# Output stage of a hybrid decoder layer: row tiles in another order of products and transposes

## Chip, core and metric

The kernel runs on one core of a Trainium2 chip. The metric is the device time of one execution in microseconds (us); the median of the runs shown is compared. Five engines work side by side, each through its own list of instructions in order: PE (TensorE, matrix products and transposes), DVE (VectorE), ACT (ScalarE), POOL (GpSimd) and SP (SyncE, which here only issues DMA transfers). An instruction that waits for a semaphore holds up everything behind it on its engine.

## The reference, cut to what matters

One layer on 1024 tokens (and 16 meta tokens) of width 1024. Two head groups, a gated delta rule (GDN) and a forgetting attention (FOX), give 512 columns each; their outputs are concatenated and go through one output projection, a residual add, an RMSNorm and a SwiGLU FFN.

```python
h = h + jnp.concatenate([o_gdn, o_fox], axis=-1) @ w_out[l]        # the output stage
h = h + swiglu(rmsnorm(h, ffn_norm_w[l]), w_gate[l], w_up[l], w_down[l])
h = rmsnorm(h, final_norm_w)
return h[:, N_META:]
```

All is float32. Each product is made of three: an operand is split into a rounded high part and the rest, and hi*hi, hi*lo and lo*hi are summed (`mm3`). `split` makes the two parts, the high one by a cast on ACT, the low one by a subtraction on DVE behind it.

## The kernel before

The stages follow each other: input projection and GDN, attention, output stage, FFN, down projection with the final norm. The change lies in the output stage and in its passage to the FFN (some 620 to 745 us of the profile below).

**The output stage** works on eight row tiles of 128 tokens, in the order `ORDER` = 0, 4, 1, 5, 2, 6, 3, 7; columns go in two halves of 512 (`nb` 0 and 1). The GDN part of half 0 is done in the attention stage for all tiles. For a tile `tt`:

- `prep_load` (L1111) loads the attention output `of` from DRAM on SP (L1113), lets POOL add its two partial halves (L1114), and lets ACT write the reciprocal row sums into the freed half (L1115).
- `prep_pe` (L1119) transposes these on PE (`rbt`, four transposes, L1125), multiplies on DVE (L1126) and splits the result into `ohl` (ACT L160, DVE L161).
- `load_h` (L1131) loads the residual `hst` on SP: for the tiles in `fused` (4, 5, 2, 6, 3, 7) one half from the input x and one from `h_d`, else all from `h_d`.
- `fox_g` (L1142) computes for a fused tile the GDN part of half 1 into the one PSUM bank `mm` (`wx`, 12 products of 128x512).
- `out_fox` (L1152) computes the FOX part, 12 products, for half 0 into `wof`, for half 1 on top of `wx` (or into `wof`). DVE adds the residual (`hst`, L1158). After half 1 comes the norm: a square sum on ACT (L1051), a scale on DVE (L205), a power on POOL (`st_f`, L206), the scaled row on DVE (`xn`, L1053).
- `u_blocks` (L1217) transposes the normed tile on PE (`u2t`, eight transposes, L1224) and splits it, or sums and differences of two tiles, into the FFN's operands `uh`, `ul` (ACT and DVE, two of the six low parts and one difference, `br`, on POOL).

Tiles have two buffers each for `of`, `hst`, `ohl` and `xn2`, so a tile's load waits until the tile two places before is done with the buffer. On PE the order is the order of the code (`tc.manual_schedule`); on the other engines a scheduler places the instructions by the code's order and its own costs. `tc.issue_after(ins)` holds back what stands in its block until `ins` has been placed.

```python
for i, tt in enumerate(ORDER):           # L1385, i = 0 is done before the loop
    if i > 1: fox_g(tt)
    out_fox(tt, 0)
    ... prep_pe(ORDER[i + 1]); load_h(ORDER[i + 1]); prep_load(ORDER[i + 2])
    out_fox(tt, 1)
    if i < NT - 1: u_blocks(ORDER[i - 1])   # at i = 7 it stands ahead of out_fox(tt, 1)
```

**Before the loop** (L1170 to L1187) tiles 0 and 4 are started: `wout_block` (L1062) loads and splits the four weight blocks of the FOX part. The last of them, `wf`, are written by ACT and DVE into memory from which the attention's last outputs `oa` are still being stored to DRAM (`o_d`). `wog` is here the GDN part of half 1 of tile 1, which is not fused; `fox_g` of tile 4 (`wx`) follows it on PE.

**The FFN** takes 11 steps `j`; a step needs seven products `p1`, `p6`, `p2`, `p7`, `p5`, `p4`, `p3` for the gate (g) and the up weights (u), with sums of weight blocks as operands. `w_ops` (L1274) makes the sums (`ws`, `s`) and splits on DVE and ACT, `ffn_bank` the products (`ga`, `ua`, `gb`, `ub`, ...: L1311, 12 each), `ffn_evict` (L1340) takes them out of PSUM (DVE L1355, `gxy`, `uxy`, `gzw`, `uzt`).

## Time and profile before

| | us |
|---|---|
| median of 3 runs | 1351.39 (1350.51 to 1355.45) |
| the profiled execution | 1359.66 |
| its span, first to last instruction | 1358.0 |
| PE busy in the span | 1312.7 (97%) |
| DVE, ACT, POOL busy | 855.4, 558.9, 430.4 |
| mean granted clock of PE | 0.983 of full speed |

The profile is one execution; the rows further down are from it. It gives for each engine when an instruction ran and what ended the idle time ahead of it. PE is busy nearly all the time, so what counts is where PE waits and where its granted clock is not 1.00; work on another engine matters where PE waits for it.

### The profile page before, as it was taken

The numbers are of one execution on the slowest core, as the hardware profiler recorded it, in microseconds if no ns is written. First come the engines' busy times: TensorE is split into PE (matmuls) and PEld (weight loads), VectorE is DVE, ScalarE is ACT, GpSimd is POOL, SyncE is SP. The second block draws the span as 40 slices with busy tenths as digits, with TensorE's granted clock in tenths as the row PEclk, the third lists the DMA queues.
The fourth block names the chain that finished last, engine by engine and source line by source line (L and its number), as shares of the span: only waits on it lengthen the run. The fifth ranks groups of instructions, "written<-read, shape, count | busy, mean of one in ns | idle before, by whom it ended". The sixth has DMA issues, their size and how long they took to land.

```text
span 1358.0 us, 20228 instructions
## 1 busy us (share of the span) xinstructions
PE 1312.7 (97%) x7442; PEld 1144.6 (84%) x7442; DVE 855.4 (63%) x1503; ACT 558.9 (41%) x930; POOL 430.4 (32%) x414
## 2 busy tenths in 40 slices
PE   8999998999999999998988999999999999999997
PEld 7999998989989877886767888888888888888886
DVE  5565677858536577994677566566655565455645
ACT  6453455322223466883444333333323343334332
POOL 2111034211022155661331654334444553010301
PEclk8999999999999998999998999999999999999999
DMA  7121536595579697846443444444455447954523
GB/s 245 57 73 53 145 113 186 164 249 168 157 271 309 172 279 206 208 114 195 146 155 117 146 171 157 160 157 164 155 171 179 165 145 254 404 224 171 199 80 124
DMA packets 192954, 237.93 MB, mean 175 GB/s; under 512 B 18896, under 2 KB 144712, under 8 KB 189144
## 3 DMA queue, kind: packets, MB, share of 16 engines
q1 hardware_dynamic: 192856, 236.65, 54.3%
q8 instruction: 58, 0.95, 0.3%
q14 instruction: 40, 0.33, 0.1%
HBM read 159.00 MB, written 77.60 MB: 174 GB/s over the span
## 4 chain that ended last, share of the span: by engine, by line
PE 80%; DMA 7%; DVE 5%; issue 3%; POOL 2%; ACT 2%; SPq 1%; POOLq 0%; DVEq 0%; ACTq 0%
PE xp L1472 8%; PE yp L1472 7%; PE ud L1311 4%; PE gd L1311 4%; PE gb L1311 4%; PE ub L1311 4%; PE ua L1311 4%; PE ga L1311 4%; PE pj_fk L200 3%; PE pj_fq L200 3%; PE ue L1311 2%; PE ge L1311 2%; PE pt L973 2%; PE fv L200 1%; PE pq L473 1%
## 5 line engine op out<-in xcount | busy, mean ns | idle before, releaser
L161 DVE TENSOR_TENSOR al_p<-ra_p,ah_p 128x2048 fp32r<-128x2048 f32 (+1 forms) x21 | 46.6, 2221 | 93.9 <-ACT ah_p L160 93.9
L926 POOL TENSOR_TENSOR bi<-ccol,cr 128x144 f32<-128x144 f32 (+7 forms) x60 | 69.7, 1166 | 55.1 <-DVE sm L942 36.1
L160 ACT CAST ah_p<-ra_p 128x2048 fp32r<-128x2048 f32 (+1 forms) x21 | 37.1, 1766 | 105.7 <-PE xp L1472 48.5
L1472 PE MATMUL xp<-wh_p,ah_p 128*128 128x512 f32 (+1 forms) x187 | 70.5, 377 | 0.7 <-DVE hs L1499 0.7
L1472 PE MATMUL xp<-wl_p,ah_p 128*128 128x512 f32 (+1 forms) x187 | 70.4, 377 | 0.0
L1472 PE MATMUL xp<-wh_p,al_p 128*128 128x512 f32 (+1 forms) x187 | 70.4, 376 | 0.0
L1360 POOL TENSOR_TENSOR gzw<-gzw,uzt 128x512 f32<-128x512 f32 x11 | 18.5, 1685 | 159.2 <-DVE uzt L1355 147.9
L1311 PE MATMUL gb<-uh_p,w_g_p 128*128 128x512 f32 x176 | 59.0, 397 | 2.9 <-DVE gxy L1355 2.9
L1360 POOL TENSOR_TENSOR gxy<-gxy,uxy 128x512 f32<-128x512 f32 x22 | 36.8, 1672 | 67.6 <-DVE uxy L1355 54.2
L1311 PE MATMUL ub<-uh_p,w_u_p 128*128 128x512 f32 x176 | 57.8, 389 | 0.0
L1311 PE MATMUL gd<-uh_p,w_g_p 128*128 128x512 f32 x176 | 57.7, 389 | 0.0
L1311 PE MATMUL ud<-uh_p,w_u_p 128*128 128x512 f32 x176 | 57.7, 389 | 0.0
L161 DVE TENSOR_TENSOR pl<-pt,ph 128x512 fp32r<-128x512 f32 (+1 forms) x96 | 51.8, 551 | 5.7 <-ACT ph L160 5.1
L161 DVE TENSOR_TENSOR w_u_p<-raw_u,w_u_p 128x512 fp32r<-128x512 f32 x42 | 41.6, 990 | 20.6 <-ACT w_u_p L160 20.5
L947 ACT ACTIVATE pr<-pr,sm 128x144 f32<-128x144 f32 (+3 forms) x64 | 50.5, 789 | 9.8 <-DVE sm L942 8.8
L160 ACT CAST ph<-pt 128x512 fp32r<-128x512 f32 (+1 forms) x96 | 45.2, 472 | 21.3 <-PE pt L973 20.8
L1311 PE MATMUL ga<-uh_p,w_g_p 128*128 128x512 f32 x160 | 52.5, 389 | 0.0
L1311 PE MATMUL ua<-uh_p,w_u_p 128*128 128x512 f32 x160 | 52.5, 389 | 0.0
L1472 PE MATMUL yp<-wh_p,ah_p 128*128 128x512 f32 x132 | 51.3, 389 | 0.0
L1472 PE MATMUL yp<-wl_p,ah_p 128*128 128x512 f32 x132 | 51.3, 389 | 0.0
L1472 PE MATMUL yp<-wh_p,al_p 128*128 128x512 f32 x132 | 51.3, 389 | 0.0
L160 ACT CAST w_u_p<-raw_u 128x512 fp32r<-128x512 f32 x42 | 26.0, 620 | 57.8 <-PE gd L1311 41.5
(629 smaller groups left out, 4350.0 us busy)
## 6 DMA issues: line engine op xcount, KB each, us to landing
ra_p<-ao_p SPq DMA_DIRECT2D x14, 1024.0 KB
raw_g<-in_w_gate_dram SPq DMA_DIRECT2D x22, 512.0 KB
raw_u<-in_w_up_dram SPq DMA_DIRECT2D x22, 512.0 KB
raw_d<-in_w_down_dram SPq DMA_DIRECT2D x22, 512.0 KB
wt_p<-raw_d SPq DMA_DIRECT2D x33, 256.0 KB
rw_p<-wt_p SPq DMA_DIRECT2D x8, 1024.0 KB
kk<-k_d SPq DMA_DIRECT2D x14, 520.0 KB
rw_p<-in_w_down_dram SPq DMA_DIRECT2D x6, 1024.0 KB
```

The lines of the kernel that those rows point to most:

```text
L160: cast = nc.scalar.copy(dst_hi, src)
L161: tail[0] = (cast, nc.vector.tensor_sub(dst_lo, src, dst_hi.bitcast(F32)))
L200: nc.tensor.matmul(dst, a, b, start=first, stop=last)
L473: nc.tensor.matmul(pq[:, 256 * i:256 * i + 256], kq[:, 0, c:c + P], kq[:, :, c:c + P], start=True, stop=True)
L926: nc.gpsimd.tensor_tensor(bi[:, :n], ccol[:, h, j:j + 1].broadcast_to([P, n]), cr[:, :n], op=ALU.subtract)
L947: nc.scalar.activation(pr[:, :n], pr[:, :n], AF.Exp, bias=sm[:, np_ - 1:np_], scale=-1.0, accum_out=rsum[:, h, j:j + 1])
L973: nc.tensor.transpose(pt[:rows_k, P * j:P * j + P], pts[j][0][:, c0:c0 + rows_k], ident)
L1311: nc.tensor.matmul(dst, a[:, c], b[:, k], start=(first and k == 0 and i == 0), stop=(k == 3 and i == 2), skip_group_check=not first)
L1360: last_mul[0] = G.tensor_tensor(gs[d], gs[d], us[d], op=ALU.mult)
L1472: nc.tensor.matmul(dst[:, n_], a[:, f, c], b[:, f, n_], start=(first and i == 0 and n == 0), stop=(i == NF - 1 and n == 2), skip_group_che ...
```

## The change

No product, transpose or transfer is added or removed. The order changes:

- Before the loop the transposes of tile 0 go ahead of `fox_g` of tile 4, those of tile 4 between the two halves of tile 0. The split of the last `wf` blocks is held back behind the split `ohl` of tile 0. The loads of `hst` for tiles 0 and 4 and of the norm's weights `nwb` are held back behind the load of `of` for tile 4.
- In the loop `fox_g(tt)` and, for the tiles from the fourth on, `u_blocks` of the tile before go between the two halves of tile `tt`.
- The first weight sums of the FFN (j = 0) are held back behind the last residual add, those of j = 1 and its first split behind the evictions of `p5` of j = 0.

```diff
     prep_load(ORDER[0])
     with tc.issue_after(last_o[0].ins):
+        prep_load(ORDER[1])
+    with tc.issue_after(ofl[ORDER[1]].ins):
         nc.sync.dma_start(nwb2, ffn_norm_w[0].partition_broadcast(P))
-    prep_load(ORDER[1])
...
-    wfs = [wout_block(4, 0), wout_block(4, 1, lambda i: [pf_tile(2 * i + c, f"wf{c}_{i}") for c in range(2)])]
+    wfs = [wout_block(4, 0)]
     rot[0] = 1
     for _ in wout_gdn(1, 1):
         pass
+    first_o = prep_pe(ORDER[0])
+    with tc.issue_after(first_o[0].ins), tc.issue_after(first_o[1].ins):
+        wfs.append(wout_block(4, 1, lambda i: [pf_tile(2 * i + c, f"wf{c}_{i}") for c in range(2)]))
+    with tc.issue_after(ofl[ORDER[1]].ins):
+        load_h(ORDER[0])
     fox_g(ORDER[1])
-    prep_pe(ORDER[0])
-    load_h(ORDER[0])
     prep_load(ORDER[2])
     out_fox(ORDER[0], 0)
+    prep_pe(ORDER[1])
+    with tc.issue_after(ofl[ORDER[1]].ins):
+        load_h(ORDER[1])
     out_fox(ORDER[0], 1)
-    prep_pe(ORDER[1])
-    load_h(ORDER[1])
     prep_load(ORDER[3])
...
+    def after_p5(j):
+        es = ExitStack()
+        for ins in p5s if j == 1 else ():
+            es.enter_context(tc.issue_after(ins.ins))
+        return es
...
-            V.tensor_tensor(s3, a11, a21, op=ALU.subtract)
-            V.tensor_tensor(a21, a21, a22, op=ALU.add)
-            V.tensor_tensor(s2, a21, a11, op=ALU.subtract)
-            V.tensor_tensor(s4, a12, s2, op=ALU.subtract)
+            with after_p5(j):
+                V.tensor_tensor(s3, a11, a21, op=ALU.subtract)
+                V.tensor_tensor(a21, a21, a22, op=ALU.add)
+                V.tensor_tensor(s2, a21, a11, op=ALU.subtract)
+                V.tensor_tensor(s4, a12, s2, op=ALU.subtract)
...
-                w_split(m, j, p, src)
+                with after_p5(j if p == "p1" else 0):
+                    w_split(m, j, p, src)
...
         for i, tt in enumerate(ORDER):
             if not i:
                 continue
-            if i > 1:
-                fox_g(tt)
             out_fox(tt, 0)
-            if i == NT - 1:
-                u_blocks(ORDER[i - 1])
-            else:
+            if i < NT - 1:
                 prep_pe(ORDER[i + 1])
                 load_h(ORDER[i + 1])
                 if 3 < i + 2 < NT:
                     prep_load(ORDER[i + 2])
+            if i > 2:
+                fox_g(tt)
+                u_blocks(ORDER[i - 1])
             out_fox(tt, 1)
-            if i < NT - 1:
+            if i < 3:
                 u_blocks(ORDER[i - 1])
...
-        first6 = {}
-        for m in "gu":
-            next(gens[m])
-            first6[m] = tail[0][1]
+        with tc.issue_after(last_h[0].ins):
+            for m in "gu":
+                next(gens[m])
```

Left out are the lines that only keep the instructions named in these blocks (`ofl` the load of `of`, `last_h` the last residual add, `p5s` the Silu of the gate's `p5` and the add of the up's).

**The start of the stage, on SP.** The number behind a name is the tile (`of_4` is tile 4), the last one only a serial number. Before:

```order
L1001 DMA o_d_108<-oa_0_7_7334 64x4x128 x2
L1113 DMA of_0_7437<-o_d_108 128x1024
L1137 DMA hst_0_7512<-h_d_5000 128x1024
L1134 DMA hst_4_7562<-in_x_dram 128x512
L1135 DMA hst_4_7562<-h_d_5000 128x512
L1001 DMA o_d_108<-oa_1_7_7414 64x4x128 x2
L1172 DMA nwb2_7436<-in_ffn_norm_w_dram 128x1024
L1083 DMA h_d_5000<-ht_1_1_7473 128x512
L1113 DMA of_4_7442<-o_d_108 128x1024
```

Now:

```order
L1113 DMA of_0_7437<-o_d_108 128x1024
L1001 DMA o_d_108<-oa_1_7_7414 64x4x128 x2
L1113 DMA of_4_7441<-o_d_108 128x1024
L1174 DMA nwb2_7436<-in_ffn_norm_w_dram 128x1024
L1083 DMA h_d_5000<-ht_1_1_7461 128x512
L1137 DMA hst_0_7499<-h_d_5000 128x1024
L1134 DMA hst_4_7541<-in_x_dram 128x512
L1135 DMA hst_4_7541<-h_d_5000 128x512
L1113 DMA of_1_7514<-o_d_108 128x1024
```

The three `hst` loads and `nwb2` stood ahead of the load of `of_4`, the `hst` loads also ahead of the last store to `o_d`; now they stand behind both.

**The same place, on ACT** (`wf0_0` and `wf0_1` are the high parts of the last weight blocks). Before:

```order
L1115 COPY of_0_7437<-rinv_96 128x512
L160 CAST wf0_0_7461<-raw_wo4_10_7463 128x1024
L160 CAST wf0_1_7467<-raw_wo4_11_7469 128x1024
L160 CAST ohl_0_7503<-of_0_7437 128x512
L1115 COPY of_4_7442<-rinv_96 128x512
```

Now:

```order
L1115 COPY of_0_7437<-rinv_96 128x512
L160 CAST ohl_0_7478<-of_0_7437 128x512
L160 CAST wf0_0_7487<-raw_wo4_10_7489 128x1024
L160 CAST wf0_1_7493<-raw_wo4_11_7495 128x1024
L1115 COPY of_4_7441<-rinv_96 128x512
```

The cast of `ohl_0` stood behind both casts of `wf0`; now it stands ahead of them.

**In the loop, on PE** (tile 5, with the transposes `u2t` of tile 1). Before:

```order
L191 MATMUL wx_5_7766<-wf1_1_7468,ohl_5_7698 128x512
L192 MATMUL wx_5_7766<-wf0_1_7467,ohl_5_7698 128x512
L1224 MATMUL u2t_1_0_7829<-ident_63,xn2_1_7728 128x128 x4
L1224 MATMUL u2t_1_1_7834<-ident_63,xn2_1_7728 128x128 x4
L190 MATMUL wx_2_7848<-whi_wo0_10_5988,uh_p5_4130 128x512
```

Now:

```order
L191 MATMUL wx_5_7796<-wlo_wo0_11_5995,uh_p4_4131 128x512
L192 MATMUL wx_5_7796<-whi_wo0_11_5994,ul_p4_4133 128x512
L1229 MATMUL u2t_1_0_7809<-ident_63,xn2_1_7728 128x128 x4
L1229 MATMUL u2t_1_1_7814<-ident_63,xn2_1_7728 128x128 x4
L190 MATMUL wx_5_7796<-wf0_0_7487,ohl_5_7698 128x512
```

The transposes of tile 1 stood behind the last product of tile 5 and right ahead of `wx` of tile 2; now they stand between the GDN products of tile 5 (with `whi_wo0`, `wlo_wo0`) and its FOX products (with `wf`), and `wx` of tile 2 comes only after its `wof`.

**The passage to the FFN, on DVE** (tiles 6, 3 and 7; `ul_p1` is an operand of `ga`, the first FFN product). Before:

```order
L1053 SCALAR_TENSOR_TENSOR xn2_3_8070<-hst_3_7974,st2_f3_8071,nwb2_7436 128x1024
L161 TENSOR_TENSOR wlo_g0_8169<-raw_g_7762,whi_g0_8168 128x512 x2
L1230 TENSOR_TENSOR ul_p3_7619<-u2t_6_1_8082,uh_p3_7618 128x4x128
L1287 TENSOR_TENSOR ws_g0_8215<-raw_g0_1_8212 128x512
L1230 TENSOR_TENSOR ul_p7_7617<-ut_6_8088,uh_p7_7616 128x4x128
L1158 TENSOR_TENSOR hst_7_8054<-wof_7_0_8117,hst_7_8054 128x512
L161 TENSOR_TENSOR wlo_u0_8175<-raw_u_7764,whi_u0_8174 128x512 x2
L1287 TENSOR_TENSOR ws_u0_8223<-raw_u0_1_8221 128x512
L1230 TENSOR_TENSOR ul_p1_7611<-u2t_3_0_8131,uh_p1_7610 128x4x128
L1288 TENSOR_TENSOR ws_g0_8215<-ws_g0_8215,raw_g_7762 128x512
```

Now:

```order
L1158 TENSOR_TENSOR hst_7_8041<-wof_7_0_8104,hst_7_8041 128x512
L161 TENSOR_TENSOR wlo_g0_8169<-raw_g_7762,whi_g0_8168 128x512
L1053 SCALAR_TENSOR_TENSOR xn2_3_8097<-hst_3_7961,st2_f3_8098,nwb2_7436 128x1024
L161 TENSOR_TENSOR wlo_g0_8169<-raw_g_7762,whi_g0_8168 128x512
L161 TENSOR_TENSOR wlo_u0_8175<-raw_u_7764,whi_u0_8174 128x512 x2
L1235 TENSOR_TENSOR ul_p1_7611<-u2t_3_0_8131,uh_p1_7610 128x4x128
L1235 TENSOR_TENSOR ul_p2_7615<-u2t_3_1_8136,uh_p2_7614 128x4x128
L1158 TENSOR_TENSOR hst_7_8041<-wx_7_8118,hst_7_8041 128x512
L1298 TENSOR_TENSOR ws_g0_8215<-raw_g0_1_8212 128x512
```

The sums `ws_g0` and `ws_u0` stood ahead of `ul_p1`; now they stand behind it and behind tile 7's last residual add.

## Rows read from the trace of the kernel before

**Rows 1.** PE's waits, 600 to 780 us: total us, times, longest.

```profile
PE wof L190 <- ACT ohl L160: 5.5, 2, 3.0
PE wx L190 <- DVE hst L1158: 3.1, 2, 2.0
PE ga L1311 <- DVE ul_p L1230: 3.0, 1, 3.0
PE gb L1311 <- DVE gxy L1355: 2.9, 1, 2.9
PE u2t L1224 <- DVE xn L1053: 1.2, 2, 0.7
PE wof L192 <- DVE ohl L161: 0.6, 1, 0.6
```

**Rows 2.** Busy us by stretch: length, PE, PEld, DVE, ACT, POOL, clock, DMA, GB/s.

```profile
631.70:634.70 3.00, 3.00 (x9) 2.35 (x8) 0.19 (x1) 0.62 (x1) 1.19 (x1) 0.50 1.16 324
...
737.30:740.70 3.40, 3.40 (x10) 2.66 (x9) 1.84 (x4) 0.00 (x0) 0.00 (x0) 0.50 0.60 169
...
620.00:743.40 123.40, 107.12 (x469) 85.16 (x470) 80.61 (x114) 52.74 (x94) 37.34 (x28) 0.93 0.49 163
```

**Rows 3.** PE's waits from 745 us to the end.

```profile
PE xp L1472 <- DVE hs L1499: 0.7, 1, 0.7
```

**Rows 4.** PE's instructions in time: start us, duration, line, out<-in, count.

```profile
622.85 0.39 PE L190 MATMUL wx<-whi_wo,uh_p 128*128 128x512 f32 x1
...
682.08 0.39 PE L190 MATMUL wof<-whi_wo,ohl 128*128 128x512 f32 x1
...
684.86 0.60 PE L1125 MATMUL rbt<-ident,of 128*128 128x128 f32 x4
685.21 0.48 PE L190 MATMUL wx<-wf,ohl 128*128 128x512 f32 x1
...
688.07 1.03 PE L1224 MATMUL u2t<-ident,xn 128*128 128x128 f32 x8
```

**Rows 5.** ACT in time; in brackets the idle time before, and releaser.

```profile
623.09 0.62 ACT L1115 COPY of<-rinv 128x512 f32<-128x512 f32 x1 [2.27 <-POOL of L1114]
...
627.63 1.04 ACT L160 CAST wf<-raw_wo 128x1024 fp32r<-128x1024 f32 x1 [2.97 <-DMA o_d<-oa]
```

**Rows 6.** SP's DMA issues in time: start us, duration of the issue.

```profile
614.80 1.23 SPq L1001 DMA_DIRECT2D o_d<-oa  x2
618.09 0.35 SPq L1113 DMA_DIRECT2D of<-o_d  x1
...
620.84 1.25 SPq L1001 DMA_DIRECT2D o_d<-oa  x2
...
627.62 0.32 SPq L1113 DMA_DIRECT2D of<-o_d  x1
```

**Rows 7.** Transfers in the chain that ended last: start us, duration.

```profile
621.49 6.08 DMA o_d<-oa
...
630.68 6.00 DMA of<-o_d
...
648.05 3.66 DMA of<-o_d
```

**Rows 8.** POOL's first add of the stage.

```profile
621.76 1.29 POOL L1114 TENSOR_TENSOR of<-of 128x512 f32<-128x512 f32 x1 [15.68 <-DMA of<-o_d]
```

**Rows 9.** DVE in time: residual add and scaled row of tile 1, scaled row of tile 5.

```profile
655.94 0.68 DVE L1158 TENSOR_TENSOR hst<-wof,hst 128x512 f32<-128x512 f32 x1
...
660.49 2.39 DVE L1053 SCALAR_TENSOR_TENSOR xn<-hst,st_f,nwb 128x1024 f32<-128x1024 f32 x1 [0.44 <-POOL st_f L206]
...
670.82 1.29 DVE L1053 SCALAR_TENSOR_TENSOR xn<-hst,st_f,nwb 128x1024 f32<-128x1024 f32 x1 [0.67 <-POOL st_f L206]
```

**Rows 10.** DVE's waits for a transfer, 600 to 780 us.

```profile
DVE ws_g L1296 <- DMA raw_g<-in_w_gate_dram: 5.0, 2, 3.1
```

**Rows 11.** Busy us in the passage to the FFN, columns as in rows 2.

```profile
703.00:743.40 40.40, 33.35 (x137) 26.28 (x136) 32.75 (x47) 17.50 (x32) 9.80 (x7) 0.92 0.38 126
```

More of the change, by code (lines that the diff above doesn't have):

```diff
@@ L1104, in tile_hymba_layer @@
     RAWS = {"g": ("hst_0", "of_0"), "u": ("xn2_0", "of_1")}
-    turn, ofs, pre_u = {}, {}, {}
+    turn, ofs, ofl, pre_u = {}, {}, {}, {}
     def wo_tile(tag, shape, bufs, nm, dt=F32, slot=None):
@@ L1112, in prep_load @@
         of = wo_tile("of", [P, 8, P], 2, tt)
-        nc.sync.dma_start(of, o_d[tt])
+        ofl[tt] = nc.sync.dma_start(of, o_d[tt])
         G.tensor_tensor(of[:, 0:4], of[:, 0:4], of[:, 4:8], op=ALU.add)
@@ L1128, in prep_pe @@
         pre_u[tt] = (oh, ol)
-        return tail[0][0]
+        return tail[0]
     def load_h(tt):
@@ L1138, in load_h @@
         pre_u[tt] += (ht,)
-    accs = {}
+    accs, last_h = {}, [None]
     def fox_g(tt):
@@ L1157, in out_fox @@
         hb = ht[:, H * nb:H * nb + H]
-        V.tensor_add(hb, acc, hb)
+        last_h[0] = V.tensor_add(hb, acc, hb)
         if nb:
@@ L1270, in halves @@
         return t[:, 0:H], t[:, WMAX // 2:WMAX // 2 + H]
-    raw0, s4s = {}, {}
+    raw0, s4s, p5s = {}, {}, []
+    def after_p5(j):
[3 more added lines that the diff above has]
+        return es
     def w_ops(v, j, m):
@@ L1354, in ffn_evict @@
             d, o = {"p6": ("y", "x"), "p7": ("x", "x"), "p5": ("z", "x"), "p3": ("y", "y"), "p4": ("x", "x")}[p]
-            V.tensor_add(t[d], b, t[o])
+            ev = V.tensor_add(t[d], b, t[o])
+            if p == "p5" and m == "u":
+                p5s.append(ev)
             if p in ("p5", "p3", "p4"):
                 if m == "g":
-                    nc.scalar.activation(gs[d], gs[d], AF.Silu)
+                    ev = nc.scalar.activation(gs[d], gs[d], AF.Silu)
+                    if p == "p5":
+                        p5s[:] = [ev]
                 else:
```

## The prediction

> **What bounds the kernel now.** I read PE's waits first, then its clock, then what holds the engine that PE waits for. In the output stage and its passage to the FFN PE waits for other engines nine times: twice for the high part of `ohl`, 5.5 us, once for its low part, 0.6; twice for the add that frees the bank `mm`, 3.1; once each for `ul_p` ahead of the first FFN product, 3.0, and for `gxy` ahead of the second `gb`, 2.9; twice for `xn`, 1.2 [rows 1]. That is 16.3 us. From 745 us on PE waits for 0.7 us in all [rows 3], so what this stage gains should reach the end of the kernel whole.
>
> The clock adds to it. Five stretches of 3.0 to 3.5 us, 16.4 us together, run at a granted clock of 0.50 or 0.51, that is 1.2 of 2.4 GHz; first and last are shown [rows 2]. Each follows one of the five waits of about 2 us and more (3.0, 2.5, 2.0, 3.0, 2.9); behind the four shorter ones none is found. At half clock a stretch does half its work, so 8.2 us more are lost. A restart costs a little as well: 12 products take 2.78 us without a gap (684.86 - 682.08 [rows 4]), 0.23 each, and the waits count from a modelled end that lies 0.16 after the point at which the next product would have begun (0.39 - 0.23). With some 0.05 for a slower first product, an estimate, that is 0.2 for each of nine waits, 1.8 us. In all 16.3 + 8.2 + 1.8 = 26.3 us of the 123.4 us stretch [rows 2] are no work. This is the most that an order can bring; the rest of the sum is what stays or comes anew.
>
> **The start of the stage.** PE is done with `wog` at 622.85 [rows 4]. Now the transposes `rbt_0` follow. They need ACT's copy into `of_0`, which ends at 623.09 + 0.62 = 623.71 [rows 5]; nothing ahead of it changes, so PE waits some 0.75 us. In return the 12 products `wx` of tile 4 (2.8 us) lie between `rbt_0` and the first product that needs `ohl_0`. The multiplication, cast and subtraction take 0.6 to 0.7 us each, as ACT's copy and DVE's add of the same size [rows 5, 9], so 2.1 us: hidden. What held the cast before was the second cast of `wf` ahead of it, which waited 2.97 us for a store to `o_d` [rows 5]. That wait is still there but stands behind `ohl_0`; who is late then is the copy for `of_4`, behind it on ACT.
>
> `of_4` must be in place when `rbt_4` comes. PE: 623.75 + 0.35 for `rbt_0`, two times 2.78, makes 629.65. Before, the load of `of_4` was issued at 627.62, since it waits for the last store to `o_d`, which took 6.08 us [rows 6, 7]. The pair of stores before it was issued by 614.80 + 1.23 = 616.03 and let the next load go at 618.09, 2.06 us later, with no load beside it [rows 6]. The `hst` loads that ran ahead of the last store now stand behind it. So I take 2.06 us: 620.84 + 1.25 + 2.06 = 624.15, then 3.66 for the load (the row at 648.05 [rows 7]), 1.29 for POOL's add [rows 8], 0.62 for ACT's copy [rows 5]: 629.75, a wait of 0.25 with latencies. The other end is a store as slow as before: 627.62 in place of 624.15, a wait of 3.7. I take the first, since its row is the same transfer without the loads ahead.
>
> `hst_0` is issued behind four transfers, at about 625.5, and lands between 3.66 and 6.00 us later [rows 7], 629.5 to 631.8. DVE's first residual add could begin at 629.85, and behind it in DVE's queue stand the multiplication and the split of tile 4. These have until 633.0, when the 12 products of tile 0's second half end; add, multiplication and cast need 2.0, so a landing by 631.0 costs nothing, one at 631.8 costs 0.8. I take 0.3.
>
> **The loop.** A steady tile is 3 x 2.78 + 0.35 + 0.9 (rows at 684.86 and 688.07 [rows 4]), some 9.6, with first products slower by 0.1 at each change 9.8 us. Between a tile's last product and the next `fox_g`, which needs the bank `mm`, now lie the 12 products of `wof` and a `rbt`, 3.1 us; DVE's add takes 0.68 [rows 9]. Both waits of 3.1 go. `ohl` gets 6 us of cover. What gets less is `xn`: `u2t` of the tile before now comes 12 + 4 + 12 products after that tile's last one, 5.9 us, where before it was some 9. The chain behind the last product is add, square sum, scale, power, scaled row. For tile 1 it took from 655.94 to 660.49 + 2.39 = 662.88, 6.9 us [rows 9]. I laid the new order on DVE, ACT and POOL out tile by tile with the durations of before. Tile 1: PE ends at T, `u2t_4` takes 0.9, so `u2t_1` is due at T + 6.8; on DVE `xn_1` stands behind the add of tile 5 and the multiplication with `rbt_2`, which ends T + 5.4, and comes to T + 6.7 with the short scaled row (1.29, tile 5) or T + 7.8 with the long one [rows 9]: a wait of 0 or 1.1 with latencies. I take 1.1, since POOL has its add and two `ul` in the same time as before. Tiles 2 and 3: POOL's power stands behind two `ul` (and for tile 2 the add of `of_7`), 0 to 1.6 each; I take 0.5 each. Tiles 5 and 6 have POOL free: 0.
>
> That long scaled row is a matter of two engines. It took 2.39 us while POOL ran and 1.29 while it did not [rows 9]. The Trainium skill (SBUF — State Buffer, SBUF: two separate sides) says that a DVE operation with two SBUF inputs and a POOL operation that reads SBUF exclude each other for a whole instruction, so the later one is blocked. The rule speaks against the change, which has `u2t` need `xn` sooner: if the overlap met tiles 2 and 3 too, they would wait 1.1 more each and the gain below would be 18.3 in place of 20.5, 1333.1 us. By the order POOL's two `ul` of tiles 2 and 3 stand ahead of the power that `xn` needs, so I expect the short row there.
>
> **The passage to the FFN.** Behind `xn_3` DVE now has three subtractions and `ul_p1`, 2.6 us; PE has `u2t_3` and 12 products, 3.7, until `ga` needs it. So the 3.0 us and their half clock go. The last norm, tile 7, keeps a wait of 0.5: its chain is as before and the cover, 24 products, too. For the first `gb`, DVE has 33 us of work in 40.4 [rows 11], some 5 of which (eight sums and splits of j = 1, 0.6 each) move behind `p5`; the time shrinks to some 33. So DVE is close to full there, and I put 0.7 (0 to 1.7) for the operand of `gb`. The wait for `gxy` ends with its cause: DVE stood 3.1 us in a weight sum whose transfer had not come [rows 10], and that sum now stands behind `p5`. What is late next would be the split for `p1` of j = 1; between its start and its use PE has four groups of 12 products, 11 us, and it takes 2 to 3, so nothing.
>
> **The sum.** What stays: 0.75 + 0.25 + 0.3 + 1.1 + 0.5 + 0.5 + 0.5 + 0.7 = 4.6, and 0.2 for each of six restarts, 1.2: 5.8. None is as long as 2 us, so no half clock. 26.3 - 5.8 = 20.5. The profiled execution took 1359.66; with 20.5 less it is 1339.2, its span 1337.5. The median is 8.3 below the profiled one, and I take the same difference: 1351.39 - 20.5 = 1330.9.
>
> **Rivals.** First, the stalls are partly the profile's own: the 8.3 us by which that execution is longer may lie in these waits, which hang on transfers. Then 20.5 - 8.3 = 12.2 are gained, 1339.2. No row says where the 8.3 lie; chance 0.10.
> Second, the last store to `o_d` stays slow: `rbt_4` waits 3.7 in place of 0.25, and 1.6 for the half clock behind it: 5.0 less, gain 15.5, 1335.9; with `hst_0` late as well 1337. Against it stands the 2.06 us of the store before [rows 6]; chance 0.13.
> Third, `xn` becomes the bound of the loop. With 6.9 to 7.8 us of chain for 5.9 of cover in all five tiles, a wait of 2 us brings the half clock with it: 5 x (2 + 1.6 + 0.2) = 19.0 in place of 2.1 + 0.6 in the sum. Gain 20.5 - 16.3 = 4.2, 1347.2. For it: DVE has `xn` behind an add of the next tile in every case. Against it: only tile 1 has both a full POOL and a long row. Chance 0.10.
> Fourth, and slower: a ring through SP. A load of `hst` waits until `xn` two tiles before has freed its buffer; the residual add with that `hst` stands ahead of the next `xn` on DVE. One turn is two issues of some 0.35 [rows 6], landing 3.66 to 6.00 [rows 7], add 0.68, `xn` 1.29 to 2.39 [rows 9]: 6.3 to 9.8 us against 9.8 for a tile on PE. It decides above 9.8. At 14.2 each of five tiles would lose 4.4 + 1.6 + 0.2, 31 us, against 23.2 gained elsewhere: 1359.2. That needs a landing of 10.4 us, and no load in this stage took over 6.0. Chance 0.04.
>
> **How the numbers follow.** Forecast 0.63, rivals 0.10, 0.13, 0.10, 0.04. The forecast's own range: with all new waits at their low ends 1.0 us stays, 1326; at their high ends some 10, 1335. With the first two rivals, and some 1 us for the spread of the medians, the range is 1325 to 1341; the third and fourth stay out. A measurement of this kernel can tell 0.5%, 6.8 us, from no change. Faster by more (below 1344.6): 0.63 + 0.10 + 0.13 = 0.86. Within: the third, 0.10. Slower: 0.04.
>
> **What would show it.** Right: no wait of `wof` for `ohl` above 1 us, no stretch at clock 0.50 from 620 us to the FFN, the load of `of` for tile 4 issued about 2 us after the last store, and the first `gd` some 20 us earlier. A wait at `rbt` near 630 us would show the second rival, waits of `u2t` for `xn` in every tile the third, DVE waiting for a load at the residual add the fourth. I am wrong if the stage shrinks and PE then waits in the FFN.

## The result and the profile after

| | before | after |
|---|---|---|
| median, us | 1353.42 (1350.51 to 1356.42) | 1339.28 (1338.54 to 1341.25) |
| the profiled execution | 1359.66 | 1338.71 |
| its span | 1358.0 | 1336.7 |
| mean granted clock of PE | 0.983 | 0.993 |
| from the first `wog` product to the first `gd`, "the stage" below | 620.03 to 743.43: 123.40 | 616.77 to 722.14: 105.37 |
| from the first `gd` to the end | 614.57 | 614.56 |

The ratio of the times is 0.9889, 95% interval 0.9864 to 0.9915: 1.1% faster, 14.1 us by the medians. The forecast was 1330.9, the range 1325 to 1341: the time lies inside, 8.4 us above the forecast. The direction was right, the size of the gain (20.5) was not. Of the 8.4 us, 2.0 are the kernel before itself (its median is 1351.39 of the three runs that the forecast started from, 1353.42 of the four here), 6.4 are gain that did not come.

PE's waits, 595 to 760 us of the changed kernel (total us, times, longest), against [rows 1]:

```profile
PE u2t L1229 <- DVE xn L1053: 2.9, 4, 1.6
PE rbt L1125 <- ACT of L1115: 2.1, 2, 1.3
PE wof L190 <- ACT ohl L160: 0.9, 1, 0.9
PE gb L1324 <- DVE ul_p L1235: 0.8, 1, 0.8
```

16.3 us have become 6.7, and no wait is as long as 2 us. The busy time of each engine in the stage (length, then PE, PEld, DVE, ACT, POOL, clock, DMA share, GB/s), against the last of [rows 2]:

```profile
616.77:722.14 105.37, 98.64 (x469) 78.78 (x470) 73.67 (x109) 53.47 (x94) 34.54 (x28) 1.00 0.57 185
```

The clock is 1.00 throughout. PE is busy for 98.64 us where the first trace of before has 107.12 for the same products; these 8.5 us are what half clock had cost. Of the 18.0 us by which the stage is shorter, 9.5 are idle time and 8.5 are clock. From 722 us on PE waits 0.7 us, as in [rows 3]; nothing is given back.

PE's instructions that still wait (start, duration, line, out<-in; in brackets the idle time before, and its releaser): tiles 0 and 4, then tiles 1, 5, 2 and 7.

```profile
620.53 0.66 PE L1125 MATMUL rbt<-ident,of 128*128 128x128 f32 x4 [0.79 <-ACT of L1115]
628.02 0.66 PE L1125 MATMUL rbt<-ident,of 128*128 128x128 f32 x4 [1.28 <-ACT of L1115]
632.39 0.50 PE L190 MATMUL wof<-whi_wo,ohl 128*128 128x512 f32 x1 [0.94 <-ACT ohl L160]
653.41 1.06 PE L1229 MATMUL u2t<-ident,xn 128*128 128x128 f32 x8 [0.51 <-DVE xn L1053]
663.77 1.06 PE L1229 MATMUL u2t<-ident,xn 128*128 128x128 f32 x8 [0.54 <-DVE xn L1053]
675.20 1.06 PE L1229 MATMUL u2t<-ident,xn 128*128 128x128 f32 x8 [1.60 <-DVE xn L1053]
703.66 1.06 PE L1229 MATMUL u2t<-ident,xn 128*128 128x128 f32 x8 [0.22 <-DVE xn L1053]
711.34 0.49 PE L1324 MATMUL gb<-ul_p,w_g_p 128*128 128x512 f32 x1 [0.81 <-DVE ul_p L1235]
```

In profiled executions the gain is 21.0 us (1359.66 - 1338.71), by the medians 14.1. The first experiments ask where the rest of these 21 lies.

### The profile page after: what moved, and what is told of

It is laid out like the page before. It is cut to its first block, busy times and chain, and to the rows that moved or that the text cites. A ratio compares the mean times of both kernels' runs of the same rounds, so it can differ in the third digit from the quotient of the medians.

```text
span 1336.7 us, 20231 instructions
## 1 busy us (share of the span) xinstructions
PE 1299.9 (97%) x7442; PEld 1134.7 (85%) x7442; DVE 849.8 (64%) x1503; ACT 558.5 (42%) x930; POOL 429.7 (32%) x414
## 4 chain that ended last, share of the span: by engine, by line
PE 83%; DMA 6%; DVE 4%; POOL 2%; issue 2%; ACT 1%; SPq 1%; POOLq 0%; DVEq 0%; ACTq 0%
PE xp L1487 8%; PE yp L1487 7%; PE gb L1324 4%; PE ud L1324 4%; PE gd L1324 4%; PE ub L1324 4%; PE ua L1324 4%; PE ga L1324 4%; PE pj_fk L200 4%; PE pj_fq L200 3%; PE ue L1324 2%; PE ge L1324 2%; PE pt L973 2%; PE fv L200 1%; PE pq L473 1%
## 5 line engine op out<-in xcount | busy, mean ns | idle before, releaser
L161 DVE TENSOR_TENSOR wl_p<-rw_p,wh_p 128x2048 fp32r<-128x2048 f32 (+1 forms) x21 | 46.9, 2235 | 3.4 <-ACT wh_p L160 3.4
```

The source lines that it names most:

```text
L161: tail[0] = (cast, nc.vector.tensor_sub(dst_lo, src, dst_hi.bitcast(F32)))
```

## The experiments

For every run the stage (first `wog` to first `gd`) of its profile, PE's busy time in it, and the ratio to the kernel before, timed on the same chip. PE's busy time is 98.6 to 98.9 us where the clock stays at 1.00; what is above is half clock.

| run | stage, us | PE busy | ratio, 95% interval |
|---|---|---|---|
| before, first trace | 123.40 | 107.12 | |
| e1_before_again | 119.02 | 103.76 | 0.9998 (0.9984 to 1.0011) |
| e2_start_only | 113.12 | 103.11 | 0.9954 (0.9937 to 0.9971) |
| e3_loop_only | 115.38 | 102.77 | 0.9962 (0.9947 to 0.9977) |
| e4_passage_only | 114.70 | 101.89 | 0.9962 (0.9949 to 0.9975) |
| after, first trace | 105.37 | 98.64 | 0.9889 (0.9864 to 0.9915) |
| e5_after_again | 104.83 | 98.64 | 0.9875 (0.9856 to 0.9893) |
| e6_loads_ahead | 105.49 | 98.58 | 0.9881 (0.9861 to 0.9900) |
| e7_xn_first | 104.55 | 98.56 | 0.9874 (0.9856 to 0.9893) |
| e8_start_inside | 106.25 | 98.70 | 0.9898 (0.9879 to 0.9917) |
| e9_loop_mended | 104.77 | 98.57 | 0.9891 (0.9870 to 0.9912) |
| e10_start_and_loop | 105.76 | 98.87 | 0.9903 (0.9882 to 0.9924) |
| e11_after_third | 105.44 | 98.67 | 0.9900 (0.9879 to 0.9921) |
| e12_wf_ahead | 108.06 | 100.54 | 0.9910 (0.9894 to 0.9927) |

### Before once more

No edit. Expected:

> The kernel before once more, unchanged: what differs from the first profile of it is execution against execution. Theory A (the 8.3 us by which the first profiled execution stood above the median lie outside the stage, in the attention before it, where that profile shows a clock of 0.94 from 500 to 560 us): the passage from the first wog product to the first gd of p5 takes 123.4 us again within 1 us, with the same five long waits, and the profiled time falls by what the attention gains, about 3 us or more. Theory B (the waits of the stage hang on transfers and were long in that one execution): the passage takes 115 to 120 us, and the wait for ohl or for gxy is shorter by several us. Time ratio to the kernel before 1.000.

The profiled execution took 1353.05 us, 6.6 less than the first one: 4.4 of them in the stage, 2.3 ahead of it (`wog` begins at 617.74 in place of 620.03; the clock from 500 to 560 us is 0.97 here, 0.94 there). The work ahead of the stage is the same in all kernels here, and `wog` begins anywhere from 614.99 to 620.03. In the stage the idle time hardly differs (15.3 against 16.3 us); what differs is the clock, 3.4 us less of busy time. The wait ahead of `gb`, and the stretch around it, show it best (columns as above):

```profile
731.21 0.47 PE L1311 MATMUL gb<-uh_p,w_g_p 128*128 128x512 f32 x1 [2.79 <-DVE gxy L1355]
```

```profile
720.00:745.00 25.00, 22.21 (x98) 18.01 (x97) 18.60 (x28) 7.65 (x14) 4.84 (x4) 1.00 0.44 137
```

The same wait, 2.91 us in the first trace, was followed there by a stretch at 0.50 [rows 2], here by none. The wait for `hst` ahead of tile 2 was 1.95 with half clock behind it, here 1.23 without. So theory B holds for the sum, though by another way than it named: not loads that came late, but half clock that came behind five waits in one execution and three in the next.

### One part at a time

The start alone:

```diff
+    first_o = prep_pe(ORDER[0])
...
+    with tc.issue_after(ofl[ORDER[1]].ins):
+        load_h(ORDER[0])
     fox_g(ORDER[1])
-    prep_pe(ORDER[0])
-    load_h(ORDER[0])
```

> The kernel before with the first part of the change alone (the order before the loop, the held-back loads of hst and nwb, the held-back split of the last wf blocks); loop and passage to the FFN as before. By the waits: away go 3.0 + 2.5 + 0.6 for ohl, 3.2 of half clock behind them and 0.6 of restarts, 9.9; new are the two waits for rbt (0.8 and 1.3), 0.9 for ohl of tile 4 and 0.6 of restarts, 3.6. So 6.3 us less, ratio 0.9953. Rival (the waits were partly the first profile's own): 3 to 4 us less, 0.997 to 0.998. Other rival (the start only hands its gain on to the loop, where xn or the loads of hst are late instead): below 2 us, and PE's waits for xn or hst behind 640 us grow.

1347.05 us against 1353.29, 6.2 less; the stage is 5.9 shorter than in the second trace of before. The sum is as expected, its place only in part: 4.4 of the 5.9 us lie at the start; the rest lies behind the first `ga`, where the wait of 2.79 us for `gxy` has become one of 0.90 at `ub`. Its two waits for `rbt` were 0.94 and 2.56 us: the load of tile 4 went out later than in the changed kernel (see the loads, below), and half clock followed.

The loop alone:

```diff
-            if i > 1:
-                fox_g(tt)
             out_fox(tt, 0)
...
+            if i > 2:
+                fox_g(tt)
+                u_blocks(ORDER[i - 1])
             out_fox(tt, 1)
```

> The kernel before with the second part alone (fox_g, and from the fourth tile on the transposes of the tile before, between the two halves of a tile). By the waits: away go 3.1 for the bank mm, 1.2 for xn, 1.6 of half clock and 0.8 of restarts, 6.7; new are four waits for xn of 2.9 together and 0.8 of restarts, 3.7. So 3.0 us less, ratio 0.998; the waits of the start (ohl) and of the passage (ul_p, gxy) stay. Rival (xn is the bound of the loop as soon as the other parts are not there): the waits for xn exceed 4 us and the time is as before or longer by 1 to 2 us.

1349.13, 4.2 less (ratio 0.9962, 5.1); the stage 3.6 shorter, where 3.0 were expected. None of it lies in the loop. There the waits for `hst` go (2.4 us in the second trace of before), but those for `xn` grow from 0.45 to 3.2, as the rival said. The gain lies behind the first `ga`: the wait of 2.9 for `ul_p` goes, with its half clock, and that for `gxy` falls from 2.79 to 0.96; the expectation had left both to the passage. Between `u2t` of tile 6 and that of tile 3 PE now has 36 products in place of 24, and DVE is done with the low parts of tile 6 ahead of `xn` of tile 3, where two of them had stood behind it. In return tile 7 waits 2.29 us, since the weight sums of j = 0 stand ahead of its norm on DVE (the scale's operand is there at 706.61, the scale runs at 708.96). Tiles 2 and 7:

```profile
680.69 1.06 PE L1224 MATMUL u2t<-ident,xn 128*128 128x128 f32 x8 [1.60 <-DVE xn L1053]
711.20 1.73 PE L1224 MATMUL u2t<-ident,xn 128*128 128x128 f32 x8 [2.29 <-DVE xn L1053]
```

The passage alone:

```diff
+            with after_p5(j):
+                V.tensor_tensor(s3, a11, a21, op=ALU.subtract)
...
+        with tc.issue_after(last_h[0].ins):
+            for m in "gu":
+                next(gens[m])
```

> The kernel before with the third part alone (the weight sums of j = 0 behind the last residual add, those of j = 1 and its first split behind the evictions of p5). By the waits: away go 3.0 for ul_p and 2.9 for gxy, 3.3 of half clock behind them and 0.4 of restarts, 9.6; new is some 0.8 + 0.2 for the operand of gb. So 8.6 us less, ratio 0.9936. Rival (the wait for gxy hangs on a transfer and was long in the first profile only): 4 to 6 us less. Other rival (what is held back is late for j = 1): the first long waits move behind 745 us, and less than 3 us are gained. If the three parts stand apart, the three gains add up to that of the whole change, 14 us by the medians, 18 by the waits.

1347.84, 5.4 less; the stage 4.3 shorter, where 8.6 were expected. The wait for `gxy` goes (2.79 us there), but it had cost no half clock in the second trace of before either; and `ga` still waits, 1.74 us, without half clock behind it:

```profile
706.44 0.50 PE L1319 MATMUL ga<-ul_p,whi_g 128*128 128x512 f32 x1 [1.74 <-DVE ul_p L1230]
```

Against the second trace of before, the three parts gain 5.9 + 3.6 + 4.3 = 13.8 us of stage, the whole change 13.6 to 14.2 (three traces). By the ratios they sum to 1.22%, the whole to 1.00 to 1.25%. But the sum hides where the gains lie. The stage in three pieces that hold the same work in all these kernels, us:

| trace | first `wog` to first `u2t` (start) | to the first `ga` (loop) | to the first `gd` (passage) |
|---|---|---|---|
| e1, before | 27.89 | 59.47 | 31.66 |
| e2, start alone | 23.49 | 59.46 | 30.17 |
| e3, loop alone | 27.83 | 59.35 | 28.20 |
| e4, passage alone | 28.02 | 59.41 | 27.27 |
| the changed kernel, three traces | 21.94, 21.29, 21.99 | 59.04, 59.17, 59.07 | 24.39, 24.37, 24.38 |

At the passage the parts overlap: 1.5, 3.5 and 4.4 us alone, 7.3 together. At the start the whole change gains 5.9 to 6.6, the first part alone 4.4. In the loop no part gains more than 0.1, the whole 0.3 to 0.4. That the sums agree is chance.

### The changed kernel again

No edit.

> The changed kernel once more, for a second trace and a closer ratio. Theory A (the new order leaves waits that hang little on transfers): the stage from the first wog product to the first gd of p5 takes 105.4 us within 1, PE's waits in it sum to 6.7 within 1, ratio 0.989 to 0.990. Theory B (what was left hangs on the loads of the start): rbt and wof differ by over 1 us between the two traces and the times spread by 4 us or more, as those of the kernel before do.

> The changed kernel a third time, as the measure for the two others: stage 104.8 to 105.5 us, waits for xn 2.8 to 3.0, ratio to the kernel before 0.988 to 0.990.

Theory A of the first, for the stage: 104.83 and 105.44 us, 2.9 and 3.0 us for `xn`, 1.60 and 1.59 of them at tile 2. The times of the first run spread by 5.0 us all the same, as theory B had it, and its ratio of 0.9875 lies below what A named; `wog` begins at 614.99 in one of the two traces and at 618.41 in the other, so at least part of that lies ahead of the stage. In the stage only the start moves: `wof` of tile 4 waited 0.94, 0.38 and 0.97. No trace of the changed kernel has half clock in the stage; before has it in both.

### The loads of hst ahead of the last store

```diff
-    with tc.issue_after(ofl[ORDER[1]].ins):
-        load_h(ORDER[0])
+    load_h(ORDER[0])
...
-    with tc.issue_after(ofl[ORDER[1]].ins):
-        load_h(ORDER[1])
+    load_h(ORDER[1])
```

> The changed kernel with the loads of hst for tiles 0 and 4 no longer held back: on SP they run ahead of the last store to o_d again, all else as changed. Theory A (loads in flight ahead of it make that store slow, 6.08 us in the first trace against 2.83 in the changed kernel): the load of of for tile 4 is issued some 6 us after the store, rbt of tile 4 waits about 4.5 us in place of 1.3, half clock behind it 1.6, against 0.9 gained since the residual is there; 3 to 4 us more than the changed kernel, ratio 0.992. Theory B (the store's time has nothing to do with the loads): the load of tile 4 is issued 2 to 3 us after the store and the time is 1 us less than the changed kernel's, since the wait of 0.9 goes.

No measurable change (0.9881 beside 0.9875 for the changed kernel on the same chip). SP's issues (start, duration): the last of the loads, the last store to `o_d`, the store of `ht`, the load of `of` for tile 4.

```profile
615.68 0.41 SPq L1135 DMA_DIRECT2D hst<-h_d  x1
616.86 1.25 SPq L1001 DMA_DIRECT2D o_d<-oa  x2
619.80 0.33 SPq L1083 DMA_DIRECT2D h_d<-ht  x1
621.84 0.33 SPq L1113 DMA_DIRECT2D of<-o_d  x1
```

From the end of the store's issue, 618.11, to the next issue that waits for it 3.73 us pass. Over all traces that gap is 5.53, 3.63, 5.49, 5.89, 3.73 and 4.78 us with the loads ahead (before, e1, e3, e4, e6, e10) and 2.83, 3.75, 2.06, 2.88, 2.00, 3.06, 2.83 and 2.00 with the loads behind (after, e2, e5, e7, e8, e9, e11, e12). So the next load goes later with the loads ahead, 4.8 against 2.7 on average, which speaks for Theory A's cause; the two ranges just meet (3.63 and 3.75), and most of these kernels differ by more than the loads. The effect did not come. `rbt` of tile 4 waits 1.29 us, as in the changed kernel, since the load of `of` itself took 3.45 us from its issue to the last update of its semaphore, in place of 3.95 to 4.05; and the residual, here early, saves the wait of `wof`. The start is 0.5 to 1.2 us shorter than the changed kernel's, the loop 1.2 to 1.3 longer (`u2t` of tile 1 waits 1.12 in place of 0.5). What POOL shows for its add of tile 4, in the changed kernel and here:

```profile
626.04 1.28 POOL L1114 TENSOR_TENSOR of<-of 128x512 f32<-128x512 f32 x1 [6.21 <-DVE wf L161]
```

```profile
625.45 1.28 POOL L1114 TENSOR_TENSOR of<-of 128x512 f32<-128x512 f32 x1 [6.22 <-DVE wf L161]
```

In both it begins 0.07 to 0.08 us after DVE's subtractions for `wf` end (625.97 and 625.37), and the profile names these as what ended the wait. They did not. The load's last semaphore update comes at 625.88 and 625.29, and the add begins 0.16 us behind it; it does so for tile 4 in every trace here, also in e5 and e8, where the subtractions still ran. But an earlier load would have gained little: in e5 the add began 0.7 us before they ended and took 1.86 us in place of 1.28, so that it ended 1.14 us behind them, in the changed kernel's first trace 1.35.

### The norm first

```diff
-        G.tensor_tensor(of[:, 0:4], of[:, 0:4], of[:, 4:8], op=ALU.add)
+        with behind(0):
+            G.tensor_tensor(of[:, 0:4], of[:, 0:4], of[:, 4:8], op=ALU.add)
...
-        V.tensor_mul(of[:, 0:4], pt, of[:, 0:4])
+        with behind(1):
+            V.tensor_mul(of[:, 0:4], pt, of[:, 0:4])
```

> The changed kernel with two more things held back in the loop: POOL's add of a tile's of behind the norm's power, and the multiplication with rbt behind the scaled row xn. Theory A (the wait of 1.6 for xn of tile 2 comes from the add of tile 7 that stands ahead of the power on POOL, that of 0.5 for tile 5 from the add of tile 3, that of 0.5 for tile 1 from DVE): the waits for xn fall from 2.9 to 0.5 us or less, with restarts 3 us less than the changed kernel, ratio 0.987. Theory B (the chain of the norm itself is too long for the cover of 28 products): the waits stay above 2 us, the time as changed. Theory C (of or ohl of the next tile comes late instead): new waits at rbt or for ohl.

The waits of tiles 1 and 5 go, that of tile 2 stays at 1.59, the low part of `ohl` of tile 2 is late by 0.39; the stage is 0.3 to 0.9 us shorter, no difference in time (0.9874). POOL and DVE at tile 2:

```profile
670.00 3.55 POOL L1240 TENSOR_TENSOR ul_p<-br,uh_p 128x512 fp32r<-128x512 f32 x2
673.51 0.55 POOL L206 TENSOR_TENSOR st_f<-st_f,mhalf 128x1 f32<-128x1 f32 x1
674.03 1.27 POOL L1118 TENSOR_TENSOR of<-of 128x512 f32<-128x512 f32 x1
```

```profile
672.41 0.15 DVE L205 TENSOR_SCALAR st_f<-st_f 128x1 f32<-128x1 f32 x1
...
674.09 2.29 DVE L1053 SCALAR_TENSOR_TENSOR xn<-hst,st_f,nwb 128x1024 f32<-128x1024 f32 x1 [0.88 <-POOL st_f L206]
```

The power's operand is there at 672.56, but two low parts hold POOL until 673.5. The add, now behind the power, begins 0.06 us ahead of the scaled row, and the row takes 2.29 us in place of 1.28. One term of the wait was exchanged for another.

### The start inside the groups of products

```diff
-    first_o = prep_pe(ORDER[0])
+    fox_g(ORDER[1], (1, lambda: first_o.extend(prep_pe(ORDER[0]))))   # behind 3 of its 12 products
...
-    prep_pe(ORDER[1])
-    out_fox(ORDER[0], 1)
+    out_fox(ORDER[0], 1, (2, lambda: prep_pe(ORDER[1])))              # behind 6 of its 12 products
```

> The changed kernel with another start: the load of hst for tile 0 right behind that of of for tile 4 (ahead of nwb and of the store of ht), the transposes of tile 0 behind the first 3 of the 12 products wx of tile 4, those of tile 4 behind the first 6 of the 12 products of tile 0's second half. Theory A (the three waits of the start, 0.8, 1.3 and 0.9 us, are gaps that products already ready can fill, the third a late residual): the sum falls from 3.0 to below 1.0, with restarts 2 to 2.5 us less than the changed kernel. Theory B (the cover taken away from ohl costs as much): wof waits for ohl by 1 to 2 us in all and the time is as changed. Theory C (of for tile 4 comes later with the residual's load beside it): rbt of tile 4 waits 1 us or more as before.

None of the three theories. The waits of the start fall from about 3 to 1.1 us (`rbt` 0.17 and 0.41, the low part of `ohl` 0.56), but `rbt` of tile 1 now waits 0.74, and `u2t` of tiles 4 and 1 wait 1.73 and 1.55; the stage is 1 us longer. POOL shows why for tile 4:

```profile
646.34 1.29 POOL L1116 TENSOR_TENSOR of<-of 128x512 f32<-128x512 f32 x1 [3.67 <-DMA of<-o_d]
647.59 0.56 POOL L208 TENSOR_TENSOR st_f<-st_f,mhalf 128x1 f32<-128x1 f32 x1
```

PE came earlier, the loads did not. The add of tile 2's `of`, which waits for its load, stands ahead of the power of tile 4 on POOL, whose operand is there at 644.55.

### Both mended

The loop as in e7, but the add of tile 7 left where it was, and further:

```diff
-        last_h[0] = V.tensor_add(hb, acc, hb)
+        with behind(1) if not nb else ExitStack():
+            last_h[0] = V.tensor_add(hb, acc, hb)
...
-        put("p4", t4, G)
+        last_put.append(lambda: put("p4", t4, G if tt == ORDER[7] else V))   # called behind out_fox(tt, 1)
```

> The changed kernel with the norm's chain put first in the loop: POOL's add of tiles 2, 6 and 3 behind the power; the multiplication with rbt and the first residual add of the next tile behind the scaled row on DVE; the last low part (p4) of tiles 4, 5 and 6 taken from POOL to DVE, behind the scaled row. Theory A (the 1.6 us at tile 2 come from POOL, where br and two low parts stood ahead of the power; with one of the low parts gone the power comes 1.3 us earlier): the waits for xn sum to 0.5 us or less in place of 2.9, stage 102.0 to 103.0 us in place of 105.1, 2 to 3 us less than the changed kernel. Theory B (the scaled row then collides with the add of tile 7 or a low part on POOL and takes 2.3 us): 1 us of the wait at tile 2 stays and the stage is 103.5 to 104. Theory C (DVE, with three more subtractions, is late elsewhere): new waits at ohl or at ga, stage as changed.

The waits for `xn` fall to 0.9 us (0.65 at tile 2, where POOL's add of tile 7, 1.83 us beside DVE, still stands ahead of the power), but DVE is late for the low part of `ohl` of tile 2 by 0.97. Stage 104.77, ratio 0.9891 beside 0.9900: no difference. Of the 2.0 us that came by Theory A, Theory C took 1.0 and the start, whose order is that of the changed kernel, 0.5.

The start as in e8, with the loads as in e6, and POOL's add of tile 1 behind the power of tile 0:

```diff
-    prep_load(ORDER[2])
+    prep_load(ORDER[2], False)      # the load alone
...
+    prep_add(ORDER[2])              # behind out_fox(ORDER[0], 1)
     prep_load(ORDER[3])
```

> As the run before, and the start anew: the loads of hst for tiles 0 and 4 ahead of the last store to o_d, as they were in the kernel before; the transposes of tile 0 behind 3 of the 12 products wx of tile 4, those of tile 4 behind 6 of the 12 of tile 0's second half; POOL's power of tile 0 ahead of the add of tile 1; the low part of ohl of tile 4 ahead of tile 0's last residual add. Theory A (the earlier try of these places failed because POOL's adds, waiting for loads, stood ahead of the powers of tiles 0 and 4, and because hst of tile 5 came late behind a longer queue of loads): the waits of the start fall from 2.5 to 3.0 us to 1.2 or less and nothing new comes behind, stage 100.5 to 102 us, 3.5 to 5 us less than the changed kernel. Theory B (the loads set the pace of the start, and PE arrives earlier only to wait for of of tile 1): a wait of 1 us or more for rbt of tile 1, stage as in the run before.

By its numbers Theory B: `rbt` of tile 1 waits. But only the wait of tile 4 is for a load; the low part of `ohl` of tile 2 waits 1.22. `rbt` of tiles 4 and 1:

```profile
631.29 0.65 PE L1136 MATMUL rbt<-ident,of 128*128 128x128 f32 x4 [1.81 <-ACT of L1127]
638.65 0.66 PE L1136 MATMUL rbt<-ident,of 128*128 128x128 f32 x4 [1.91 <-ACT of L1127]
```

POOL ahead of the second:

```profile
636.16 0.56 POOL L208 TENSOR_TENSOR st_f<-st_f,mhalf 128x1 f32<-128x1 f32 x1 [5.57 <-DVE st_f L207]
636.68 1.26 POOL L1126 TENSOR_TENSOR of<-of 128x512 f32<-128x512 f32 x1
```

The load of tile 1 had its last semaphore update at 632.83. POOL stood idle until 636.16, for the power of tile 0, and the add was held behind it by this edit. So whether the loads set the pace of the start was not tested here.

Stage 105.76. No version tried is better than the changed kernel by more than a measurement can tell.

### The split of wf ahead again

```diff
-    wfs = [wout_block(4, 0)]
+    wfs = [wout_block(4, 0), wout_block(4, 1, lambda i: [pf_tile(2 * i + c, f"wf{c}_{i}") for c in range(2)])]
...
-    with tc.issue_after(first_o[0].ins), tc.issue_after(first_o[1].ins):
-        wfs.append(wout_block(4, 1, lambda i: [pf_tile(2 * i + c, f"wf{c}_{i}") for c in range(2)]))
```

> The changed kernel with the split of the last wf blocks no longer held back: on ACT and DVE it stands ahead of the split ohl of tile 0 again, as in the kernel before, while PE keeps the new order (12 products wx between rbt of tile 0 and the first product that needs ohl). In the profiles of the changed kernel the last store to o_d ends some 2 to 3.8 us after its issue, so the second cast of wf, which waits for it, would end about 1.2 us after rbt of tile 0 is done and 1.5 us ahead of the first wof; the cast of ohl follows, its low part behind two subtractions of wf on DVE. Theory A (the PE order alone takes the cast out of the way): wof waits 0 to 1 us for ohl of tile 0, nearly all for the low part, and the time is at most 1 us above the changed kernel's. Theory B (the queue behind the store is what cost 5.5 us before, and the cover of 2.8 us is too short for it): a wait of 2 us or more for the high part with half clock behind it, 3 to 5 us more than the changed kernel, ratio 0.992.

At the place itself Theory A: `wof` waits 0.64 us, for the low part alone. The order of PE by itself takes the cast out of the way. Yet the stage is 2.9 us longer than the changed kernel's (108.06 in one trace against 105.2, the mean of three). The ratio, 0.9910 (0.9894 to 0.9927) against 0.9875 to 0.9900, hardly tells the two apart: its interval overlaps those of two of the three runs of the changed kernel. The cost comes 12 us later, with half clock behind it:

```profile
639.97 0.66 PE L1125 MATMUL rbt<-ident,of 128*128 128x128 f32 x4 [3.02 <-ACT of L1115]
```

```profile
640.00:645.00 5.00, 5.00 (x18) 3.99 (x19) 3.40 (x3) 1.24 (x2) 1.03 (x1) 0.66 0.26 97
```

`of` of tile 1 shares its buffer with tile 0's, which is free only after the low part of `ohl` of tile 0. That ends here at 626.48 + 0.69 = 627.17, behind the two subtractions for `wf`. On SP the scheduler set the two weight loads ahead of the load of tile 1, which is issued at 629.76, some 10.5 us after the stage's start; in the changed kernel at 625.21, 8.4 us after:

```profile
626.89 0.52 SPq L1269 DMA_DIRECT2D raw_g<-in_w_gate_dram  x1
627.46 2.13 SPq L1269 DMA_DIRECT2D raw_u<-in_w_up_dram  x1
629.76 5.02 SPq L1113 DMA_DIRECT2D of<-o_d  x2
```

The buffer alone does not explain it: it is free 7.9 us after the stage's start, ahead of the issue in the changed kernel. The order on SP does, and only the place of the split differs between the two kernels; why the scheduler turned the order is not shown. So the held-back split is worth its place in this trace, but not for the product that it stood ahead of: for the load of tile 1.

## Why the prediction was right or wrong

**The cause.** Right for the start and the passage. Waits and the half clock behind them were the loss, the new order takes the long ones away, and nothing comes back in the FFN. The clock was put at 8.2 us and gave 8.5 against the first trace, 5.1 against the second. In the loop the order mainly exchanged one wait for another: 2.4 us for `hst` in the second trace, 2.7 to 2.8 for `xn` ahead of the first `ga` in the changed kernel. There it gains 0.3 to 0.4 us; the 2.7 against the first trace are mostly the half clock behind its wait of 1.95.

**The base.** Wrong, and this is the larger part of the miss. The sum was made against the first profiled execution; "and I take the same difference" carried its 8.3 us above the median over to the changed kernel. The second trace of before has 4.4 us less in this stage (3.4 of them clock) and 2.3 less ahead of it. Against it the change gains 13.6 us of stage, close to the 14.1 of the medians. The first rival said this, at 1339.2; 1339.28 was measured. It was given 0.10, because no row told where the 8.3 lay. Its reason was off as well: the part in the stage was mostly half clock, which followed a wait of 2.91 us in one execution and not one of 2.79 in the next, far more than late transfers. That the changed kernel's profiled execution, 1338.71, came so near the 1339.2 that the sum gives for it is luck: the stage lost 18.0 us and not 20.5, and 3.3 us came from ahead of the stage, where nothing was changed.

**What stays.** 4.6 us were predicted, 6.7 measured. Term by term, over three traces:

- `rbt` of tile 0: 0.75 predicted, 0.79, 0.88 and 0.74 measured.
- `rbt` of tile 4: 0.25 predicted, 1.28, 1.08 and 1.30 measured (the four terms give 629.72, not 629.75). The store took 2.83 in the first trace and the third, not the 2.06 of the pair before it, and POOL's add began 4.12 us after the load's issue in place of 3.66. In the second trace the store took the 2.06, but there the add ran beside DVE's subtraction for `wf`, which the change itself had put there, and took 1.86 in place of 1.29.
- `hst` of tile 0: 0.3 predicted, 0.94, 0.38 and 0.97 measured. The load took 7.06, 7.16 and 7.03 us, behind four other transfers, beyond the 6.00 that was the upper end. "No load in this stage took over 6.0" was a misreading: in the first trace of before the second half of `hst` of tile 4 was issued at 619.65 and had its last semaphore update at 626.88, 7.23 us later. The load in the chain, and DVE's row:

```profile
623.25 7.06 DMA hst<-h_d
630.40 0.69 DVE L1158 TENSOR_TENSOR hst<-wof,hst 128x512 f32<-128x512 f32 x1 [4.43 <-DMA hst<-h_d]
```

- `xn`: 2.6 predicted for the four terms of `u2t`, 2.9 measured, differently shared: tile 1 about 0.5 in place of 1.1, tile 2 1.60 in place of 0.5, tile 3 none, tile 5 0.5 to 0.7 in place of none, tile 7 0.22 in place of 0.5. Tile 2 came at the upper end that was given. POOL, when the power's operand was ready at 671.0:

```profile
670.14 1.83 POOL L1114 TENSOR_TENSOR of<-of 128x512 f32<-128x512 f32 x1
671.93 1.29 POOL L1235 TENSOR_TENSOR ul_p<-br,uh_p 128x512 fp32r<-128x512 f32 x1
673.19 0.54 POOL L206 TENSOR_TENSOR st_f<-st_f,mhalf 128x1 f32<-128x1 f32 x1
```

- The operand of `gb`: 0.7 predicted, 0.81 measured; `ga` and `gxy` none, as predicted.

The long scaled row met no tile: all eight took 1.27 to 1.28 us. The reading of [rows 9] was half right: beside the short row of tile 5 POOL had an add too, but it began later, at 671.68, and it was the add that took longer, 1.56 us. What counts is which comes first. In the changed kernel the row for tile 1 was the first of the two, and POOL's add beside it paid (2.17 in place of 1.29 us):

```profile
651.98 1.27 DVE L1053 SCALAR_TENSOR_TENSOR xn<-hst,st_f,nwb 128x1024 f32<-128x1024 f32 x1
```

```profile
652.23 2.17 POOL L1114 TENSOR_TENSOR of<-of 128x512 f32<-128x512 f32 x1 [2.06 <-ACT uh_p L1234]
```

In e7 the add began first and the row took 2.29. That is what the Trainium skill (SBUF — State Buffer, SBUF: two separate sides) states: the later of the two is blocked. These rows agree with it in both directions.

**The rivals.** The second (the store stays slow) did not come in the changed kernel, where the gap behind the store is 2.06 to 2.83 us; in e2 it came in part, with 3.75 us and a wait of 2.56 for `rbt` of tile 4. The third (`xn` as the loop's bound) did not come at its price, with waits of 2.9 in all and none of 2 us, but those waits took back nearly all that the loop had to gain. The fourth (a ring through SP) did not, though in e12 another order on SP made a load late, 3.0 us at one tile.

## What to carry to other kernels

Before an order is costed from one trace, take a second trace of the kernel before: here 4.4 of 123 us differed between two executions of the same program, most of it clock. Where a transpose waits for a row that another engine makes, list what stands ahead of each link of that chain on each engine; an add that itself waits for a load must not stand ahead of a power that is ready (e8), nor an add whose load has landed behind a power that is not (e10). When parts of a change are tried one by one, compare the places of their gains and not only the sums. And look past the product that a moved instruction delays: a load that goes later because of it may cost more.

## What was not expected of the hardware

- Half clock did not follow the length of a wait alone: it came behind 1.95 us at `wx` (the first trace) and 2.29 at `u2t` (e3), and behind 1.49 and 1.64 together, 2.4 us apart, at `wof` (e1), not behind 1.81 and 1.91 at `rbt` (e10) nor behind 2.79 at `gb` (e1). Nor did it last equally long: some 3.5 us behind `ga` in the two traces of before, over 6.5 there in e2, behind the same wait. What decides was not looked into.
- The pair of last stores took 2.00 to 3.75 us with no load of the residual ahead of it and 3.63 to 5.89 with such loads ahead, at the same size.
- POOL's add of tile 4 took 1.86 and 2.21 us in place of 1.28 where it began beside DVE's subtraction for `wf` (e5, e8). In four other traces (after, e6, e7, e11) it began 0.04 to 0.09 us behind that subtraction, which the profile then names as the releaser; its load's last semaphore update, 0.16 us ahead of the add in all of them, says that it was the load.
